# A recurrent branch whose heads overlap: a head's outputs are made inside the next head, and its squares are summed by two products of rounded numbers

## The chip, the cores and the metric

The kernel runs on one core of a Trainium2 chip as one program. The metric is the device time of one execution in microseconds (us), and lower is better. A core has a matrix engine (TensorE, "PE" in the profile), a vector engine (VectorE, "DVE"), an engine for functions of one operand (ScalarE, "ACT"), GpSimd ("POOL"), and SyncE ("SP"), whose queue starts most transfers here.

## The reference, cut to what matters

One encoder block on 512 tokens of width 1024: a mixer of two branches, then a retrieval layer (PEER) over 16384 small experts. The change is in the recurrent branch (HGRN2) of the mixer, which has 8 heads of 128 channels. Of its computation this much is touched:

```python
    o = o2[:B] + rev(o2[B:])                                  # both directions of the recurrence
    o = rmsnorm(o, hgrn_norm_g).reshape(B, L, HGRN_WIDTH)     # over the 128 channels of a head
    y_a = jnp.einsum('blc,cd->bld', (o * jax.nn.silu(og.astype(f32))).astype(xn.dtype), w_branch_a)

def rmsnorm(x, g):
    xf = x.astype(jnp.float32)
    y = xf * lax.rsqrt(jnp.mean(xf * xf, axis=-1, keepdims=True) + RMS_EPS)
    return (y * g.astype(jnp.float32)).astype(x.dtype)
```

The outputs `o` of a head are sums of products: scores with values within a chunk of 128 tokens, and queries with the states carried from the chunks before and after.

## The kernel before, in words

Tokens lie along the free axis (512 columns), channels along the 128 partitions. Products of full precision are made of three products of rounded numbers: `split` makes a rounded copy (`hi`, by ACT, line 94) and the rest (`lo`, by DVE, line 95), and `mm3` (lines 103, 104, 106) multiplies hi by hi, lo by hi and hi by lo. A projection of the input by one block of 128 columns of a weight is 24 such products of 128x512; this is called a block below. The first 16 of a block read `whi`, the last 8 `wlo`, and each of the two has two buffers, so the rest `wlo` of a weight can be written only when the block two before it has ended.

The function `hgrn` runs the recurrent branch. For every head `scores` makes the decays: two scans `Z` (699, 700), the keys and queries to the ends of the chunks `KE` and `QE` (719 to 724), transposes of the keys (733), states `S` (745, 752, 754), and, in two groups of levels, tiles `Dt`: a difference of `Z` (787, 788, DVE), its exponent (790, ACT), a product with keys and queries (769, 770, DVE). The products of each group (692, PE) give the score tiles `near` and `sct` (818, 825). Then `outputs` (835 to 841) multiplies the scores by the values `vh` and the queries by the states, into the PSUM tile `po`, and squares it; `normed` (847 to 851) adds up the squares over the channels by a product with a matrix of ones and scales the head. `sigmoids` of the next head is emitted within `scores`.

Beside this, PE makes five blocks per head, for the heads that come: `queried` and `forgets` (two each, run by `beside` between the steps of `scores`) and `values`. `weave` lets `beside` advance as `scores` yields costs. In the first step of `beside`, the norm of the head before and the transposes of the values (654) are emitted.

The code's order is not the order on the engines: when the program is built, a scheduler places the emitted instructions into one order per engine, with estimates of its own. On the chip every engine takes its instructions in that order and waits at one whose input or buffer isn't ready. So a change to what is emitted where can move instructions on all engines.

## Time and profile before

| | us |
|---|---|
| median of three runs | 2030.59 |
| lowest, highest | 2029.78, 2035.2 |
| profiled execution | 2031.44 |
| its span, first to last instruction | 2029.3 |
| recurrent branch, from head 0's outputs to the end of its last blocks | 405.6 to about 700 |
| busy in 405.6 to 700: PE, DVE, ACT | 289.9, 241.9, 209.8 |

A row of the profile names a line of the code, the engine, the operation, and the tiles as out<-in. In a list in order of time the first two numbers are the start and the length in us, and in brackets stands how long the engine was idle before it and whom it waited for. A product of two F32 tiles shows as two rows of half the work each, a product of rounded tiles as one row; the type reads f32 for both. The granted clock of TensorE is 1.00 in all of the stretch from 405.6 to 700.

### The profile page before, as it was taken

How to read it: one execution, taken by the hardware profiler on the slowest of the kernel's cores; microseconds unless marked ns; L12 is line 12 of the kernel's file. 1: busy time of each engine (PE TensorE's matmuls, PEld its weight loads, DVE VectorE, ACT ScalarE, POOL GpSimd, SP SyncE). 2: the span in 40 equal slices, each digit the busy share in tenths (PEclk: the TensorE clock that was granted, in tenths of full speed). 3: DMA queues.
4: the chain of work that ended last, by engine and by line, in shares of the span. 5: the costliest groups of instructions: out<-in, count | busy, mean ns of one | idle time of the engine just before them, and what ended most of it. 6: DMA issues, size and time to landing. Idle time of an engine off the chain costs nothing.

```text
span 2029.3 us, 32589 instructions
## 1 busy us (share of the span) xinstructions
PE 2005.8 (99%) x12553; PEld 1772.1 (87%) x12553; DVE 1656.0 (82%) x3016; ACT 983.7 (48%) x1473; POOL 555.4 (27%) x331
## 2 busy tenths in 40 slices
PE   8999999999999999999999999999999999999998
PEld 6788888888887888889999998888888888888887
DVE  6788863888988647979999968887897889898895
ACT  5555443777775623436767743333333323333333
POOL 0000000000000000000000027776766767766760
PEclk9999999999999999999999999999999999999999
DMA  5212113222212434214767998888988898998884
GB/s 187 94 53 68 63 58 108 84 74 74 69 70 73 138 144 146 99 68 154 228 203 234 276 339 327 327 333 317 362 312 315 319 361 338 367 346 328 325 306 156
DMA packets 160409, 418.08 MB, mean 206 GB/s; under 512 B 12890, under 2 KB 66012, under 8 KB 160126
## 3 DMA queue, kind: packets, MB, share of 16 engines
q1 hardware_dynamic: 115180, 263.58, 37.1%
q0 software_dynamic: 36864, 134.23, 18.0%
q10 hardware_dynamic: 8210, 18.19, 2.6%
q8 instruction: 98, 1.61, 0.3%
q14 instruction: 57, 0.47, 0.1%
HBM read 377.94 MB, written 38.01 MB: 205 GB/s over the span
## 4 chain that ended last, share of the span: by engine, by line
PE 94%; DVE 2%; issue 1%; DMA 1%; ACT 1%; POOL 0%; ACTq 0%; DVEq 0%; POOLq 0%
PE ps_mm L103 11%; PE ps_mm L104 10%; PE ps_mm L106 10%; PE ps_a L104 8%; PE ps_a L103 8%; PE ps_a L106 8%; PE acc L1132 8%; PE acc L1131 8%; PE acc L1133 8%; PE ps_g L1418 4%; PE ps_x L103 1%; PE ps_x L106 1%; PE ps_x L104 1%; PE ps_x L692 1%; PE ps_s L1263 1%
## 5 line engine op out<-in xcount | busy, mean ns | idle before, releaser
L103 PE MATMUL ps_a<-pxh,uh 128*128 128x384 f32 x1024 | 346.8, 339 | 0.4 <-ACT gact L983 0.4
L95 POOL TENSOR_TENSOR ul<-uraw,uh 128x1024 fp32r<-128x1024 f32 x70 | 186.4, 2663 | 576.1 <-PE ps_a L106 435.5
L104 PE MATMUL ps_a<-pxl,uh 128*128 128x384 f32 x1024 | 343.9, 336 | 0.0
L1132 PE MATMUL acc<-vl,gh 128*128 128x512 f32 x768 | 299.9, 390 | 0.0
L1131 PE MATMUL acc<-vh,gh 128*128 128x512 f32 x768 | 299.4, 390 | 0.0
L1133 PE MATMUL acc<-vh,gl 128*128 128x512 f32 x768 | 299.3, 390 | 0.0
L94 ACT CAST vh<-vraw 128x1024 fp32r<-128x1024 f32 x128 | 134.6, 1052 | 309.5 <-DMA vraw<-in_v 177.8
L103 PE MATMUL ps_mm<-xh,whi 128*128 128x512 f32 (+1 forms) x656 | 256.7, 393 | 0.4 <-ACT gt L265 0.4
L104 PE MATMUL ps_mm<-xl,whi 128*128 128x512 f32 (+1 forms) x656 | 252.6, 387 | 0.0
L1074 DVE SCALAR_TENSOR_TENSOR grow<-grow,xg 128x1024 f32<-128x1024 f32 x128 | 196.2, 1551 | 51.1 <-DMA grow<-in_u,gidx 50.7
L1086 DVE SCALAR_TENSOR_TENSOR xg<-grow,gw,xg 128x1024 f32<-128x1024 f32 x127 | 197.5, 1555 | 25.9 <-DMA grow<-in_v,gidx 23.5
L954 POOL IOTA iota<- 128x512 bf16 x1 | 1.2, 1189 | 764.3 <-PE ps_mm L106 764.3
L1045 POOL DMA_INDIRECT grow<-in_u,gidx x128 | 194.4, 1518 | 42.2 <-issue 23.4
L106 PE MATMUL ps_a<-pxh,ul 128*128 128x384 f32 x1024 | 198.3, 334 | 0.0
L103 PEld LDWEIGHTS ps_a<-pxh,uh 128*128 128x128 f32 x1024 | 192.4, 188 | 4.2 <-ACT gact L983 1.2
L104 PEld LDWEIGHTS ps_a<-pxl,uh 128*128 128x128 f32 x1024 | 192.7, 188 | 3.4
L95 DVE TENSOR_TENSOR wlo<-wraw,whi 128x1024 fp32r<-128x1024 f32 x112 | 136.5, 1220 | 71.2 <-ACT whi L94 41.5
L95 DVE TENSOR_TENSOR vl<-vraw,vh 128x1024 fp32r<-128x1024 f32 x128 | 182.5, 1426 | 5.3 <-ACT vh L94 5.3
L94 ACT CAST whi<-wraw 128x1024 fp32r<-128x1024 f32 x112 | 117.5, 1049 | 136.6 <-PE ps_mm L104 127.2
L94 ACT CAST uh<-uraw 128x1024 fp32r<-128x1024 f32 x128 | 134.5, 1051 | 101.3 <-PE ps_a L104 71.6
L1045 POOL DMA_INDIRECT grow<-in_v,gidx x128 | 173.3, 1354 | 37.0 <-issue 21.7
L106 PEld LDWEIGHTS ps_a<-pxh,ul 128*128 128x128 f32 x1024 | 179.3, 188 | 0.0
(420 smaller groups left out, 3988.8 us busy)
## 6 DMA issues: line engine op xcount, KB each, us to landing
uraw<-in_uT SPq DMA_DIRECT2D x128, 512.0 KB
vraw<-in_v SPq DMA_DIRECT2D x128, 512.0 KB
wraw<-in_w_in SPq DMA_DIRECT2D x80, 512.0 KB
Gd<-Gs SPq DMA_DIRECT2D x12, 2048.0 KB
gt<-Gd SPq DMA_DIRECT2D x32, 768.0 KB
kept<-gact ACTq DMA_DIRECT2D x22, 384.0 KB
gkept<-kept SPq DMA_DIRECT2D x22, 384.0 KB
wraw<-in_w_q SPq DMA_DIRECT2D x16, 512.0 KB
```

The lines of the kernel that those rows point to most:

```text
L94: nc.scalar.copy(hi, src)
L95: return (eng or nc.vector).tensor_sub(lo, src, hi).ins
L103: nc.tensor.matmul(out, ah, bh, start=(i == 0), stop=False)
L104: nc.tensor.matmul(out, *((al, bh) if late else (ah, bl)), start=False, stop=False)
L106: nc.tensor.matmul(out, *((ah, bl) if late else (al, bh)), start=False, stop=(stop and i == n - 1))
L1045: nc.gpsimd.indirect_dma_start(out=t, out_offset=None, in_=tab, in_offset=bass.IndirectOffsetOnAxis(ap=gidx[:, j : j + 1], axis=0))
L1074: nc.vector.scalar_tensor_tensor(t, t, 1.0, xg, op0=ALU.mult, op1=ALU.mult, accum_out=gdot[h][:, i : i + 1])
L1086: nc.vector.scalar_tensor_tensor(gacc, t, gw[h][:, i : i + 1], gacc, op0=ALU.mult, op1=ALU.add)
L1131: nc.tensor.matmul(acc[k][c], gh[:, ts_], vh[:, ds_], start=(r == 0), stop=False)
L1132: nc.tensor.matmul(acc[k][c], gh[:, ts_], vl[:, ds_], start=False, stop=False)
L1133: nc.tensor.matmul(acc[k][c], gl[:, ts_], vh[:, ds_], start=False, stop=(r == NK - 1))
L1418: nc.tensor.matmul(pg[:, q * P : q * P + P], own[:, q], rows[:, q], start=True, stop=True)
```

## The change

Three things change. First, `outputs` of a head is no longer emitted after `values` of the next one, but inside the next head, in the first step of `beside`, after that step's first block and before the transposes of the values. Second, the norm moves to the second step of `beside`. Third, the squares are split into a rounded part and a rest, which take a buffer of the ring of six `Dt` tiles, and the F32 product with ones becomes two products of rounded tiles with a constant `unit`. (`st[hd] = [raw]` is set earlier, which emits nothing.)

```diff
+    unit = cp.tile([P, P], F32R, name="unit")
+    nc.vector.memset(unit.bitcast(F32), 1.0)
...
         o2 = w1.tile([P, L], F32, name="o2")
         nc.scalar.activation(o2, po, AF.Square)
-        st[hd] += [po, o2]
+        o = w2.tile([P, 2, L], F32R, name="o2s", tag="Dt", bufs=6)
+        oh, ol = o[:, 0], o[:, 1]
+        split(nc, oh, ol, o2)
+        st[hd] += [po, oh, ol]
 
     def normed(hd):
-        so, po, o2 = st[hd][1], st[hd][-2], st[hd][-1]
+        so, (po, oh, ol) = st[hd][1], st[hd][-3:]
         pm = C.ps_x.tile([P, L], F32, name="ps_x")
-        nc.tensor.matmul(pm, C.ones, o2, start=True, stop=True)
+        nc.tensor.matmul(pm, unit, oh, start=True, stop=False)
+        nc.tensor.matmul(pm, unit, ol, start=False, stop=True)
...
     def beside(hd, work):
 
-        for i, c in enumerate(work):
+        for i in range(4):
+            if i == 1 and hd:
+                normed(hd - 1)
+            c = next(work)
             if i == 0:
                 if hd:
-                    normed(hd - 1)
+                    outputs(hd - 1)
                 transposed(hd)
             yield c
...
         weave(scores(hd), beside(hd, work), per)
         if hd < HEADS - 1:
             values(hd + 1)
-        outputs(hd)
+    outputs(HEADS - 1)
```

Lines from 618 on move down by two in the changed kernel, and from 845 on by more: the outputs are at 837, 839 and 841, the squares at 843, the products with `unit` at 852 and 853.

What this moves on the engines is shown for a middle head. On PE, before, the outputs (835 to 839) stand ahead of the transposes of the next head's keys (733), and the norm (847) comes one block after these:

```order
L839 MATMUL ps_x<-QE,S 128x128
L835 MATMUL ps_x<-sct,vh 128x128
L837 MATMUL ps_x<-QE,S 128x128
L733 MATMUL ps_x<-ident,KE 128x128 x6
L103 MATMUL ps_mm<-xh,whi 128x512
L104 MATMUL ps_mm<-xl,whi 128x512
```

In the changed kernel the transposes (735 now) stand four products into the next block:

```order
L103 MATMUL ps_mm<-xh,whi 128x512
L104 MATMUL ps_mm<-xl,whi 128x512
L735 MATMUL ps_x<-ident,KE 128x128 x6
L103 MATMUL ps_mm<-xh,whi 128x512
L104 MATMUL ps_mm<-xl,whi 128x512
```

and the outputs follow when that block has ended:

```order
L106 MATMUL ps_mm<-xh,wlo 128x512 x8
L837 MATMUL ps_x<-sct,vh 128x128
L841 MATMUL ps_x<-QE,S 128x128
L837 MATMUL ps_x<-sct,vh 128x128
L839 MATMUL ps_x<-QE,S 128x128
```

So the outputs of a head now come 20 products and six transposes after the keys of the next head are ready, instead of ahead of the transposes.

On DVE, before, the work on the first `Dt` tiles of a head stands around the product that ends `KE` (723):

```order
L709 TENSOR_TENSOR tot<-Z,lf 128x4
L780 COPY Dt<-KQ 128x512
L781 TENSOR_TENSOR Dt<-KQ,Dt 128x512
L95 TENSOR_TENSOR wlo<-wraw,whi 128x1024
L818 COPY_PREDICATED near<-masks,ps_x 128x256
L723 TENSOR_TENSOR KE<-KQ,KE 128x2x384
L818 COPY_PREDICATED near<-masks,ps_x 128x256
L724 TENSOR_TENSOR QE<-KQ,QE 128x768
L818 COPY_PREDICATED near<-masks,ps_x 128x256
L787 TENSOR_TENSOR Dt<-Z 128x8x64
L788 TENSOR_TENSOR Dt<-Z 128x2x4x64
L787 TENSOR_TENSOR Dt<-Z 128x16x32
```

Now two rests of weights stand ahead of it, and the rest of the squares (`o2s`) ahead of most of it:

```order
L677 MEMSET lf 128x2
L725 TENSOR_TENSOR KE<-KQ,KE 128x2x384
L726 TENSOR_TENSOR QE<-KQ,QE 128x768
L95 TENSOR_TENSOR wlo<-wraw,whi 128x1024 x2
L782 COPY Dt<-KQ 128x512
L789 TENSOR_TENSOR Dt<-Z 128x8x64
L95 TENSOR_TENSOR o2s<-o_4540,o2s 128x512
L783 TENSOR_TENSOR Dt<-KQ,Dt 128x512
L790 TENSOR_TENSOR Dt<-Z 128x2x4x64
L789 TENSOR_TENSOR Dt<-Z 128x16x32
```

Only a copy and one difference of the new head's `Dt` work are left between the keys and the rest of the squares; all else on the levels comes behind the squares of the head before. The order of the transfers on SP's queue and of the work on POOL is the same in both kernels.

## The prediction

> **What bounds the kernel now.** I read the busy shares first, then the recurrent branch by stretches from one head's outputs to the next, then PE's, DVE's and ACT's rows in order of time there. The page's first part, and five stretches of one head each (columns: stretch, length, then busy time and count of PE, PE's weight loads, DVE, ACT, POOL; clock; DMA):

> ```profile
> PE 2005.8 (99%) x12553; PEld 1772.1 (87%) x12553; DVE 1656.0 (82%) x3016; ACT 983.7 (48%) x1473; POOL 555.4 (27%) x331
> ...
> 442.54:479.50 36.96, 36.31 (x420) 29.90 (x420) 32.27 (x56) 27.72 (x43) 0.00 (x0) 1.00 0.21 72
> ...
> 590.45:627.33 36.88, 36.24 (x422) 29.81 (x421) 32.16 (x55) 27.64 (x43) 0.00 (x0) 1.00 0.22 73
> sum 184.79, PE 181.64 PEld 149.62 DVE 161.33 ACT 138.57 POOL 0.00; mean PE 36.33 PEld 29.92 DVE 32.27 ACT 27.71 POOL 0.00
> ```

> PE fills the whole kernel, so a change in one stage reaches the end whole. A head takes 36.96 us (184.79 / 5). DVE is busy for 32.27 of it: a second engine, 4.7 us below the bound. PE's rows at two head ends, and the wait named there:

> ```profile
> 402.36 1.97 PE L106 MATMUL ps_mm<-xh,wlo 128*128 128x512 f32 x8
> 405.61 0.49 PE L835 MATMUL ps_x<-sct,vh 128*128 128x128 f32 x2 [1.27 <-ACT sct L825]
> ...
> 439.94 1.98 PE L106 MATMUL ps_mm<-xh,wlo 128*128 128x512 f32 x8
> 442.54 0.49 PE L835 MATMUL ps_x<-sct,vh 128*128 128x128 f32 x2 [0.62 <-ACT sct L825]
> ...
> 444.65 0.39 PE L837 MATMUL ps_x<-QE,S 128*128 128x128 f32 x2
> 444.87 0.82 PE L733 MATMUL ps_x<-ident,KE 128*128 128x128 f32 x6
> 445.45 0.47 PE L103 MATMUL ps_mm<-xh,whi 128*128 128x512 f32 x1
> 445.76 0.40 PE L104 MATMUL ps_mm<-xl,whi 128*128 128x512 f32 x1
> 445.99 0.40 PE L103 MATMUL ps_mm<-xh,whi 128*128 128x512 f32 x1
> ...
> 451.01 1.02 PE L847 MATMUL ps_x<-o,ones 128*128 128x512 f32 x2
> 451.87 0.60 PE L654 MATMUL ps_x<-ident,vT 128*128 128x128 f32 x4
> ```

> Starts count, since PE overlaps its rows. Products of 128x512 start 0.23 apart (445.76, 445.99), so after eight from 439.94 the outputs could start at 441.77; they start at 442.54, a loss of 0.77. At head 0 it is 405.61 less 404.19, 1.42. The F32 product with ones takes 0.86 (451.01 to 451.87). A block takes 5.56 (445.45 to 451.01), the transposes of the keys 0.58, the outputs 2.50 from first start to last end (442.54 to 445.04).

> **The change part by part.** *Two rounded products for one of F32:* 2 x 0.23 for 0.86, so 0.40 less on PE, eight times. No row has `unit` as an operand; the nearest rows are the block's own products of this size, the other end is 0.86 each, as the F32 product (+0.86 per head). I take 0.23, the same kind.

> *Outputs one block later:* ACT's copies of `sct` are then long done, and the wait of 0.77 goes. Were PE alone the limit, a head would take 36.96 - 0.77 - 0.40 = 35.8.

> *What is late next:* DVE. In the new order its rows from the rest of the squares (`o2s`) of one head to the keys `KE` of the next stand without a gap to fill, and the next `o2s` can't start until those keys have gone through PE, a block, the outputs, and ACT. That is a loop, and I add up one turn of it. DVE's rows (groups of the stretch 442.5 to 479.5 with mean ns; rows of other stages for a split of 128x512; rows in order of time):

> ```profile
> L95 DVE TENSOR_TENSOR wlo<-wraw,whi 128x1024 fp32r<-128x1024 f32 x5 | 6.1, 1219 | 2.1 <-ACT whi L94 1.5 <-issue 0.7
> L787 DVE TENSOR_TENSOR Dt<-Z 128x512 f32<-128x512 f32 x6 | 4.1, 681 | 0.0
> L724 DVE TENSOR_TENSOR QE<-KQ,QE 128x768 f32<-128x768 f32 x1 | 0.9, 939 | 0.0
> L780 DVE COPY Dt<-KQ 128x512 f32<-128x512 f32 x1 | 0.5, 497 | 0.0
> ...
> L95 DVE TENSOR_TENSOR mgl<-gt,mgh 128x512 fp32r<-128x512 f32 x8 | 5.5, 685 | 1.1 <-ACT mgh L94 1.1
> L94 ACT CAST mgh<-gt 128x512 fp32r<-128x512 f32 x8 | 5.0, 620 | 12.2 <-DVE gt L306 12.2
> ...
> 442.13 0.68 DVE L788 TENSOR_TENSOR Dt<-Z 128x512 f32<-128x512 f32 x1
> 442.73 0.68 DVE L787 TENSOR_TENSOR Dt<-Z 128x512 f32<-128x512 f32 x1
> 443.33 0.68 DVE L788 TENSOR_TENSOR Dt<-Z 128x512 f32<-128x512 f32 x1
> 443.93 1.22 DVE L95 TENSOR_TENSOR wlo<-wraw,whi 128x1024 fp32r<-128x1024 f32 x1
> 445.07 0.68 DVE L769 TENSOR_TENSOR Dt<-KQ,Dt 128x512 f32<-128x512 f32 x1
> ```

> The starts lie 0.08 closer than the lengths (0.60 for a row of 0.68, 1.14 for the rest of a weight). The split adds 0.60 on DVE: 32.27 + 0.60 = 32.87 of work per head. Behind `KE` and so outside the run stand `QE` (0.86), two rests of weights (2.28), the copy (0.42) and one difference (0.60): 4.16. The run is 28.71 of work.

> [...]

> Waits inside the run, from ACT's rows:

> ```profile
> L779 ACT ACTIVATE Dt<-lf 128x512 f32<-128x512 f32 x1 | 0.9, 887 | 0.3 <-PE ps_x L692 0.3
> ...
> 445.84 0.59 ACT L841 ACTIVATE o<-ps_x 128x512 f32<-128x512 f32 x1
> ...
> 452.66 0.58 ACT L656 COPY vh<-ps_x 128x512 f32<-128x512 f32 x1
> 453.12 0.64 ACT L125 ACTIVATE hrs<-hrs 128x512 f32<-128x512 f32 x1
> ...
> 472.98 0.53 ACT L721 ACTIVATE KE<-Z 128x384 f32<-128x384 f32 x1 [1.54 <-DVE Z L700]
> 473.82 0.19 ACT L711 ACTIVATE edec<-tot 128x8 f32<-128x8 f32 x1
> 474.51 0.98 ACT L719 ACTIVATE KE<-Z,tot 128x128 f32<-128x128 f32 x3
> 478.63 0.82 ACT L825 COPY sct<-near 64x256 f32<-64x256 f32 x2 [2.26 <-DVE near L818]
> ```

> Behind the split, DVE's next row needs ACT's exponent of 0.89, which starts with the split and outlasts its step of 0.60 by some 0.2. Before `KE`, ACT now does an exponent (0.53), two copies of `sct` (0.82), `edec` (0.19) and three exponents (0.98) after the second scan, about 2.2 with steps overlapping, while DVE has only some 1.7 to do (a masked copy, two tiny ones, a rest of a weight at 1.14): 0.5 idle. With 0.2 for other handovers, 0.9. It could be 0.3, if the copies come early, or 1.6. The run is 29.6.

> From `KE` to the next `o2s`: PE's transposes 0.58, 20 products, which are a block less four (5.56 - 0.92 = 4.64), outputs 2.50, two handovers of 0.05: 7.8. ACT's square and copy of `vh` (0.46 to 0.48 apart by the starts above), the cast at 0.62 and a handover: 1.6. One turn: 29.6 + 7.8 + 1.6 = **39.0 to 39.1 us**, against 36.95 for the same turn before. I use 39.1. In those 9.4 us DVE has 4.16 of work and stands some 4.7 to 5.2 idle, first at the second rest of a weight (its buffer comes free when the block ends), then at `o2s`; differences of the new head, whose scans are done, are queued behind both. PE waits for DVE: it needs 35.8 and gets 39.1, so 3.3 per head, at the products of the second group of levels and at the transposes of the keys.

> Six turns, from head 0's outputs to head 6's; the rows of these before (the chain of waits):

> ```profile
> 405.61 0.49 PE ps_x L835 x2
> ...
> 627.33 0.49 PE ps_x L835 x2
> ```

> Before: 221.72, or 36.95 each. Added: 6 x (39.1 - 36.95) = 12.9. At the start the first outputs come later by transposes and a block, less the wait that goes: 0.58 + 5.56 - 1.42 = +4.7. At the end these lie ahead of head 6's outputs and need not follow: -6.1, and two norms are 0.40 shorter: -0.8. Head 7's outputs stay where they were. **Sum: 12.9 + 4.7 - 6.9 = +10.7 us.**

> *The rest:* setting `unit` is one small write by DVE at the head of the stage, where 0.7 of slack per head hides it, 0.2 at most if not. The split's 0.62 on ACT lies in the loop and is counted. Transfers of weights keep their order and start when buffers free, later with the loop; no transfer is added. The retrieval layer's work follows PE's and moves as a whole, since its gathers start from PE's projections there too.

> The profiled execution took 2031.44 (span 2029.3), 0.85 over the median of 2030.59: by it 2042.1, by the median 2041.3. I give the latter.

> **The rivals.** *PE stays the bound, faster.* If DVE's work for the second group were done when PE gets there, PE would lose nothing anew: waits of 1.42 and six of about 0.75 go, eight norms give 3.2, about -9: 2021.5. For it speaks PE's 99%; against it, that DVE has 4.7 idle per head before, and the new order alone takes that much between `KE` and `o2s`. It decides if a turn is under 35.8, 3.3 shorter than my sum. No wait in the run and none of the handovers make half of that. Chance 6%.

> *About even.* A turn of 36.95 + (6.9 - 4.7) / 6 = 37.3 leaves the time unchanged, and 36.3 to 38.3 keeps it within 6 us, 0.3% (about what a measurement of this kernel can tell from no change). That needs 0.8 to 2.8 less than my sum, for instance DVE's steps for rows on PSUM shorter, or the handovers less. Chance 8%.

> *ACT late as well.* ACT gains a cast (0.52 as a step) on 27.71 busy, and two weight casts stand back to back in front of the transposes' copies. If ACT's in-order queue held `KE` or the exponents 1 to 2 us more per turn, the time would be 6 to 12 us longer: 2047 to 2053. Against it: ACT has 9 us idle per head. Chance 7%. [...]

> **How the numbers follow.** My case, +6 to +16, has 78%, and its likeliest value is 2041.3. The waits in the run, 0.3 to 1.6 against 0.9, are -3.6 to +4.2 over six turns; with the handovers this is 2036 to 2047, where about 8 in 10 lie, the upper edge of the even case and the lower of ACT's included. Slower by over 0.3%: 78 + 7 + 1 = 86%; within 0.3%: 8%; faster: 6%.

> **What would show it.** Right: starts of the outputs (837) some 39 us apart in heads 1 to 6; PE's waits for `sct` gone; PE waiting for DVE at 694's second group (about 2 us a head) and at 735 (some 0.5); DVE idle before `wlo` and before `o2s`, together 4 to 5 us a head; the products with `unit` 0.23 apart; the retrieval layer as long as before. Wrong: no wait of PE at 694, which is the first rival; or DVE's idle time moved into the run, with ACT named, which is the third.

## The result, and the profile after

The changed kernel takes **2050.49 us** (median of 4 runs, 2049.99 to 2051.82) against 2032.22 for the kernel before in the same comparison. The ratio is 1.0095, with a 95% interval of 1.0081 to 1.0109: slower, as forecast, but by 18.3 us (medians) and not by 10.7. The profiled execution has a span of 2048.7 us against 2029.3 before, 19.4 more, and this is the amount taken apart here.

The engines' busy time (the page's first part) and six stretches, each from one head's outputs to the next head's (called a turn below; columns as in the prediction's first list):

```profile
PE 2014.0 (98%) x12553; PEld 1776.0 (87%) x12553; DVE 1659.8 (81%) x3025; ACT 989.7 (48%) x1481; POOL 557.5 (27%) x331
```

```profile
409.24:449.00 39.76, 36.70 (x421) 29.93 (x420) 33.41 (x56) 28.00 (x43) 0.00 (x0) 1.00 0.20 67
449.00:490.53 41.53, 39.21 (x421) 31.97 (x420) 33.38 (x56) 28.12 (x43) 0.00 (x0) 0.92 0.19 64
490.53:530.27 39.74, 36.76 (x422) 30.01 (x421) 33.30 (x56) 28.01 (x43) 0.00 (x0) 1.00 0.20 68
530.27:572.11 41.84, 39.65 (x421) 32.17 (x420) 33.38 (x56) 28.12 (x43) 0.00 (x0) 0.92 0.19 64
572.11:612.09 39.98, 36.88 (x421) 30.00 (x420) 33.31 (x56) 28.15 (x43) 0.00 (x0) 1.00 0.19 67
612.09:652.72 40.63, 38.04 (x421) 30.82 (x420) 33.38 (x55) 28.02 (x43) 0.00 (x0) 0.96 0.19 66
sum 243.48, PE 227.23 PEld 184.91 DVE 200.17 ACT 168.41 POOL 0.00; mean PE 37.87 PEld 30.82 DVE 33.36 ACT 28.07 POOL 0.00
```

Two things are to be seen. A turn now takes 39.7 to 40.0 us where the clock is full, 0.6 to 0.9 over the 39.1 that the prediction's loop through DVE has. And three of the six turns are longer still, and in just these the granted clock (third number from the end) is below 1.00. The forecast had no such term.

The 19.4 us between the spans are divided at three rows of PE: the transposes of head 0's keys, the first outputs and head 6's outputs. First the kernel before (its outputs at 405.61 and 627.33 stand in the prediction), then the changed one, both from PE's rows in order of time:

```profile
371.26 0.82 PE L733 MATMUL ps_x<-ident,KE 128*128 128x128 f32 x6
```

```profile
370.24 0.82 PE L735 MATMUL ps_x<-ident,KE 128*128 128x128 f32 x6
...
409.24 0.39 PE L837 MATMUL ps_x<-sct,vh 128*128 128x128 f32 x2
...
652.72 0.27 PE L837 MATMUL ps_x<-sct,vh 128*128 128x128 f32 x1
```

| piece | before, us | after, us | measured | forecast |
|---|---|---|---|---|
| up to head 0's transposes | 371.26 | 370.24 | -1.0 | 0 |
| from there to the first outputs | 34.35 | 39.00 | +4.65 | +4.7 |
| six turns | 221.72 | 243.48 | +21.76 | +12.9 |
| from head 6's outputs to the end | 1401.97 | 1395.98 | -6.0 | -6.9 |
| sum | 2029.3 | 2048.7 | +19.4 | +10.7 |

So 8.9 us more than forecast lie in the six turns; the other differences, -1.0 and +0.9, nearly cancel.

**An undisturbed turn.** DVE's rows in order of time (brackets: idle time ahead, and what ended it), from the outputs of 490.53 to those of 530.27:

```profile
490.79 1.23 DVE L95 TENSOR_TENSOR wlo<-wraw,whi 128x1024 fp32r<-128x1024 f32 x1 [3.10 <-PE ps_mm L106]
491.93 0.50 DVE L782 COPY Dt<-KQ 128x512 f32<-128x512 f32 x1
492.35 0.68 DVE L789 TENSOR_TENSOR Dt<-Z 128x512 f32<-128x512 f32 x1
494.59 0.69 DVE L95 TENSOR_TENSOR o2s<-o,o2s 128x512 fp32r<-128x512 f32 x1 [1.56 <-ACT o2s L94]
495.37 0.69 DVE L783 TENSOR_TENSOR Dt<-KQ,Dt 128x512 f32<-128x512 f32 x1
495.98 0.68 DVE L790 TENSOR_TENSOR Dt<-Z 128x512 f32<-128x512 f32 x1
...
498.63 0.69 DVE L771 TENSOR_TENSOR Dt<-KQ,Dt 128x512 f32<-128x512 f32 x1 [0.16 <-ACT Dt L792]
...
513.81 0.69 DVE L771 TENSOR_TENSOR Dt<-KQ,Dt 128x512 f32<-128x512 f32 x1 [0.31 <-ACT Dt L792]
...
523.97 0.96 DVE L725 TENSOR_TENSOR KE<-KQ,KE 128x768 f32<-128x768 f32 x1 [0.80 <-ACT KE L721]
```

DVE stands idle for 3.10 and 1.56 between one head's keys and the rest of its predecessor's squares, 4.7 together, while the new head's differences stand queued behind. From `o2s` at 494.59 to the end of `KE` at 524.93 the run takes 30.34. Then PE needs 5.34 until the outputs start (530.27). The outputs before had started at 490.53; ACT's square follows them 2.44 later and the rest of the squares another 1.62:

```profile
492.97 0.60 ACT L843 ACTIVATE o<-ps_x 128x512 f32<-128x512 f32 x1 [3.00 <-PE ps_x L839]
493.46 0.58 ACT L658 COPY vh<-ps_x 128x512 f32<-128x512 f32 x1
493.93 0.63 ACT L94 CAST o2s<-o 128x512 fp32r<-128x512 f32 x1
```

30.34 + 5.34 + 2.44 + 1.62 = 39.74, the whole turn. PE waits at the second group of products (694) and at the keys (735), as these waits of PE from 400 to 700 us show (total, times, longest):

```profile
PE ps_x L694 <- ACT raw L637: 6.7, 5, 1.5
PE ps_x L694 <- DVE Dt L772: 4.3, 6, 0.7
PE ps_x L735 <- DVE KE L725: 1.8, 3, 0.6
```

The wait for `sct` of before is gone. The profile puts the longest of these waits down to ACT's copy of `raw`, since that ends last, 0.06 before the products start (in the sixth head it names another copy of ACT's, `ga`). But in each of the six heads these products start 0.15 after DVE's row 772 has ended, which makes their operand, and so do those of the second line, put down to DVE. Both are waits for DVE.

**A disturbed turn.** PE's rows at the second group of products in the turn from 449.00 to 490.53:

```profile
470.65 1.52 PE L106 MATMUL ps_mm<-xh,wlo 128*128 128x512 f32 x6
473.72 0.46 PE L694 MATMUL ps_x<-Dt 128*32 128x32 f32 x32 [1.55 <-ACT raw L637]
474.92 0.66 PE L694 MATMUL ps_x<-Dt 128*32 128x32 f32 x32 [0.74 <-DVE Dt L772]
...
478.37 0.63 PE L103 MATMUL ps_mm<-xh,whi 128*128 128x512 f32 x1
478.80 0.63 PE L104 MATMUL ps_mm<-xl,whi 128*128 128x512 f32 x1
...
481.67 0.39 PE L103 MATMUL ps_mm<-xh,whi 128*128 128x512 f32 x1
481.89 0.39 PE L104 MATMUL ps_mm<-xl,whi 128*128 128x512 f32 x1
```

Behind the waits of 1.55 and 0.74, products of 128x512 start 0.43 apart (478.37, 478.80), and from 481.67 on 0.22 apart again. The clock's records in the trace say the same: half from 474.68 for 6.83 us, from 556.60 for 6.83, and from 638.52 for 3.41, full otherwise until the very end of the kernel. The first of these stretches, as a row of the kind shown above:

```profile
474.68:481.51 6.83, 6.56 (x76) 4.88 (x77) 6.03 (x12) 2.91 (x5) 0.00 (x0) 0.50 0.23 79
```

The kernel before has no half clock in this stage.

### The profile page after: what moved, and what is told of

It is laid out like the page before. It is cut to its first block, busy times and chain, and to the rows that moved or that the text cites. A ratio compares the mean times of both kernels' runs of the same rounds, so it can differ in the third digit from the quotient of the medians.

```text
span 2048.7 us, 32590 instructions
## 1 busy us (share of the span) xinstructions
PE 2014.0 (98%) x12553; PEld 1776.0 (87%) x12553; DVE 1659.8 (81%) x3025; ACT 989.7 (48%) x1481; POOL 557.5 (27%) x331
## 3 DMA queue, kind: packets, MB, share of 16 engines
q1 hardware_dynamic: 115180, 263.58, 36.5%
q8 instruction: 99, 1.62, 0.3%
## 4 chain that ended last, share of the span: by engine, by line
PE 91%; ACT 5%; DVE 3%; DMA 1%; issue 0%; SPq 0%; ACTq 0%; DVEq 0%
PE ps_mm L103 9%; PE ps_mm L104 9%; PE ps_mm L106 9%; PE ps_a L104 9%; PE ps_a L103 9%; PE ps_a L106 9%; PE acc L1141 9%; PE acc L1140 9%; PE acc L1142 9%; PE ps_g L1427 4%; PE ps_x L103 1%; PE ps_x L106 1%; PE ps_x L104 1%; PE ps_s L1272 1%; ACT Dt L792 1%; PE ps_x L747 1%
## 5 line engine op out<-in xcount | busy, mean ns | idle before, releaser
L95 POOL TENSOR_TENSOR ul<-uraw,uh 128x1024 fp32r<-128x1024 f32 x70 | 190.1, 2716 | 578.5 <-PE ps_a L106 433.9
L103 PE MATMUL ps_a<-pxh,uh 128*128 128x384 f32 x1024 | 346.8, 339 | 0.3 <-ACT gact L992 0.3
L104 PE MATMUL ps_a<-pxl,uh 128*128 128x384 f32 x1024 | 343.9, 336 | 0.0
L94 ACT CAST vh<-vraw 128x1024 fp32r<-128x1024 f32 x128 | 134.5, 1051 | 266.7 <-DMA vraw<-in_v 136.4
L103 PE MATMUL ps_mm<-xh,whi 128*128 128x512 f32 (+1 forms) x656 | 259.8, 398 | 1.6 <-ACT whi L94 0.9
L104 PE MATMUL ps_mm<-xl,whi 128*128 128x512 f32 (+1 forms) x656 | 255.9, 392 | 0.0
L1083 DVE SCALAR_TENSOR_TENSOR grow<-grow,xg 128x1024 f32<-128x1024 f32 x128 | 190.1, 1505 | 51.3 <-DMA grow<-in_u,gidx 51.0
L1095 DVE SCALAR_TENSOR_TENSOR xg<-grow,gw,xg 128x1024 f32<-128x1024 f32 x127 | 201.7, 1588 | 30.9 <-DMA grow<-in_v,gidx 29.2
L1054 POOL DMA_INDIRECT grow<-in_u,gidx x128 | 193.0, 1508 | 39.7 <-issue 22.2
L106 PE MATMUL ps_a<-pxh,ul 128*128 128x384 f32 x1024 | 198.3, 334 | 0.0
L104 PEld LDWEIGHTS ps_a<-pxl,uh 128*128 128x128 f32 x1024 | 192.7, 188 | 3.5
L103 PEld LDWEIGHTS ps_a<-pxh,uh 128*128 128x128 f32 x1024 | 192.4, 188 | 3.7 <-ACT gact L992 0.6
L95 DVE TENSOR_TENSOR wlo<-wraw,whi 128x1024 fp32r<-128x1024 f32 x112 | 136.6, 1220 | 71.1 <-PE ps_mm L106 40.0
L94 ACT CAST uh<-uraw 128x1024 fp32r<-128x1024 f32 x128 | 134.5, 1051 | 114.6 <-PE ps_a L104 82.8
L106 PEld LDWEIGHTS ps_a<-pxh,ul 128*128 128x128 f32 x1024 | 179.3, 188 | 0.0
L95 DVE TENSOR_TENSOR vl<-vraw,vh 128x1024 fp32r<-128x1024 f32 x128 | 175.8, 1374 | 3.2 <-ACT vh L94 3.2
L94 ACT CAST whi<-wraw 128x1024 fp32r<-128x1024 f32 x112 | 116.7, 1047 | 124.6 <-PE ps_mm L104 112.6
```

Source lines behind the costliest of these rows:

```text
L94: nc.scalar.copy(hi, src)
L95: return (eng or nc.vector).tensor_sub(lo, src, hi).ins
L103: nc.tensor.matmul(out, ah, bh, start=(i == 0), stop=False)
L104: nc.tensor.matmul(out, *((al, bh) if late else (ah, bl)), start=False, stop=False)
L106: nc.tensor.matmul(out, *((ah, bl) if late else (al, bh)), start=False, stop=(stop and i == n - 1))
L1054: nc.gpsimd.indirect_dma_start(out=t, out_offset=None, in_=tab, in_offset=bass.IndirectOffsetOnAxis(ap=gidx[:, j : j + 1], axis=0))
```

## The experiments

Theory: the loss is the loop of the prediction, and it closes (its members wait for one another all the way round) because two things come together. `o2s` takes a buffer of the ring of six that the `Dt` tiles use, and buffers of a ring are handed out in the order of the code, so the new head's `Dt` work stands behind `o2s` on DVE; and the outputs, a block later than before, make `o2s` late. The idle time that this gives PE lowers the clock (to half for 6.83, 6.83 and 3.41 us, by the records above), on top. Rivals: one part alone costs the time, or the clock alone does.

### One part alone: the split, with the outputs at their old place

```diff
-        for i in range(4):
-            if i == 1 and hd:
-                normed(hd - 1)
-            c = next(work)
+        for i, c in enumerate(work):
...
-                    outputs(hd - 1)
+                    normed(hd - 1)
...
-    outputs(HEADS - 1)
+        outputs(hd)
```

> Two rounded products and the split, with outputs and norm left where they were before the change. Theory (the loss needs both parts: outputs that stand behind a block, and the rest of the squares in the ring of Dt tiles, which puts the new head's Dt work behind it on DVE): a turn of some 36.1 us, PE full, 5 to 9 us faster than before. Rival 1 (the split costs, since DVE and ACT each get a row more per head): 3 to 12 us slower. Rival 2 (the move alone costs): 3 us faster, eight norms at 0.40.

Measured: 2024.91 us (2023.49 to 2026.03) against 2030.03; ratio 0.9974 (0.9965 to 0.9983), faster. Five of the six turns take 36.3 to 36.4, one 37.8, and the six 219.73 against 221.72 before, with a full clock:

```profile
402.32:622.05 219.73, 215.39 (x2521) 179.60 (x2519) 197.39 (x335) 168.47 (x259) 0.00 (x0) 1.00 0.22 73
```

### The other part alone: the outputs a block later, squares summed whole

From the changed kernel, with the sum of the kernel before:

```diff
-        o = w2.tile([P, 2, L], F32R, name="o2s", tag="Dt", bufs=6)
-        oh, ol = o[:, 0], o[:, 1]
-        split(nc, oh, ol, o2)
-        st[hd] += [po, oh, ol]
+        st[hd] += [po, o2]
...
-        nc.tensor.matmul(pm, unit, oh, start=True, stop=False)
-        nc.tensor.matmul(pm, unit, ol, start=False, stop=True)
+        nc.tensor.matmul(pm, C.ones, o2, start=True, stop=True)
```

> Outputs inside the next head and the norm in its second step, but with the one F32 product with ones and no split. Theory (both parts needed): the wait for the score copies goes, a turn of some 36.3 us, 4 to 6 us faster than before, clock at 1.00 throughout. Rival 1 (the split costs): also 4 to 6 faster. Rival 2 (the move alone costs, since the outputs come a block later in the loop): 10 to 20 us slower.

Measured: 2025.25 us (2024.57 to 2026.36); ratio 0.9977 (0.9968 to 0.9986), faster. The turns are 36.3 to 36.5, and the start (39.03) and the end (1395.9) as in the changed kernel. The six turns:

```profile
409.23:627.19 217.96, 217.87 (x2522) 179.93 (x2521) 192.65 (x329) 166.26 (x252) 0.00 (x0) 1.00 0.22 74
```

So neither part costs anything by itself: each gives about 5 us, and both together cost 18 to 19.

### Both parts, the split in another buffer

```diff
-        o = w2.tile([P, 2, L], F32R, name="o2s", tag="Dt", bufs=6)
+        o = w1.tile([P, 2, L], F32R, name="o2s", tag="KE")
```

> The changed kernel with one edit: the split squares take the buffer of KE in place of one of the six Dt buffers; same instructions. Theory (the ring of Dt hands out buffers in the order of the code, so new Dt work can't go ahead of the split squares): DVE's Dt work moves ahead again, a turn of about 36 us, 6 to 9 us faster than before, no wait of PE at the second group, clock at 1.00. Rival (the outputs' place behind a block and DVE's extra row make the loop long, wherever the buffer is): as the changed kernel, 17 to 20 us slower than before.

Measured: 2024.34 us (2023.73 to 2026.21); ratio 0.9975 (0.9964 to 0.9985): 5.7 us faster than before, a little under the 6 to 9 expected. Six turns take 217.30 with a full clock, so this one line is worth 26.6 us by the spans (2022.1 and 2048.7). DVE's rows at the same place in the program show why:

```profile
473.05 0.95 DVE L725 TENSOR_TENSOR KE<-KQ,KE 128x768 f32<-128x768 f32 x1
...
475.45 0.50 DVE L782 COPY Dt<-KQ 128x512 f32<-128x512 f32 x1
475.87 0.67 DVE L783 TENSOR_TENSOR Dt<-KQ,Dt 128x512 f32<-128x512 f32 x1
...
485.38 0.68 DVE L772 TENSOR_TENSOR Dt<-KQ,Dt 128x512 f32<-128x512 f32 x1
485.98 0.67 DVE L95 TENSOR_TENSOR o2s<-o,o2s 128x512 fp32r<-128x512 f32 x1
```

Between the keys and `o2s` DVE now works for 12 us without a gap, on 14 rows of the new head's `Dt` among others (the first and the last two are shown), where the changed kernel had two of them and 4.7 us idle. The loop is open; no row became cheaper.

### The clock alone: PE kept busy in its waits

Five rounded products ahead of the second group in heads 1 to 6; the group overwrites what they put in its bank, so their values are not used:

```diff
             bank = C.ps_x.tile([P, L], F32, name="ps_x")
+            if 0 not in levels and 0 < hd < HEADS - 1:
+                for _ in range(5):
+                    nc.tensor.matmul(bank, xh[:, 0, :P], xh[:, 1], start=True, stop=True)
```

> The changed kernel with five more products of rounded 128x512 tiles (about 1.15 us) put on PE ahead of the second group of levels in heads 1 to 6, into the PSUM tile that the group then overwrites; their values are not used. Theory (PE's idle stretch there lowers the granted clock to half for 3.4 to 6.8 us in three heads, which costs 4.5 us in all): clock at 1.00 throughout, every turn about 39.8 us, 3 to 5 us faster than the changed kernel, 14 to 16 us slower than before. Rival (the clock has another cause, or the products are not hidden): as the changed kernel or up to 7 us slower than it, 19 to 26 us slower than before.

Measured: 2045.67 us (2044.54 to 2046.15); ratio 1.0076 (1.0062 to 1.0089). The clock is full throughout, and the turns are 39.76, 39.77, 39.79, 39.78, 39.77 and 39.77. Their sum, in one stretch:

```profile
409.13:647.76 238.63, 226.95 (x2551) 185.30 (x2550) 200.04 (x335) 168.16 (x258) 0.00 (x0) 1.00 0.20 67
```

That is 4.85 below the changed kernel's 243.48, with 30 products more on PE. So the half clock costs 4.85 us, and 39.77 is the loop's own turn (238.63 / 6): PE's five products per head lie in its waits and cost nothing.

The same with two products in place of five:

> The changed kernel with two 128x512 rounded products in heads 1 to 6, issued to PE ahead of the second group, whose values nobody uses; the run with five of them held the clock at 1.00. They leave PE idle for some 1.8 of 3.4 us at that place. If the clock falls only where PE idles for about two thirds of such a stretch (2.2 us, as in the changed kernel), it stays at 1.00 and the kernel takes 2045 to 2047 us with turns of 39.8. If half a stretch is enough, some turns are again 0.8 to 2 us longer with clock records of 0.5, and the time is 2048 to 2051 us.

Measured: 2048.26 us (2047.8 to 2050.96); ratio 1.0090 (1.0076 to 1.0104). The mean clock is 0.96 in four turns, which is what 3.41 us at half make of 40.5 us (1 - 0.5 x 3.41 / 40.5), and these take 40.4 to 40.6; the other two have 1.00 and take 39.77. So the first theory of that run, that two thirds of a stretch must be idle, falls. In the changed kernel's records a drop lasts 3.413 us or 6.827, twice as long, and the drops begin 81.92 us apart, 24 times 3.413; in this run the first two and the last two of the four begin 40.96 apart, 12 times 3.413. So I divided the time into stretches of 3.41 that end where the drops begin, and read PE's busy time. The changed kernel (three that a drop follows, then the one with least PE work that none follows):

```profile
471.26:474.67 3.41, 1.37 (x37) 0.79 (x35) 3.09 (x6) 3.41 (x6) 0.00 (x0) 1.00 0.00 0
553.18:556.59 3.41, 1.44 (x66) 0.83 (x64) 3.09 (x7) 3.41 (x5) 0.00 (x0) 1.00 0.00 0
635.10:638.51 3.41, 1.14 (x65) 0.79 (x64) 3.13 (x6) 3.41 (x5) 0.00 (x0) 1.00 0.00 0
512.21:515.62 3.41, 1.88 (x39) 1.30 (x37) 3.10 (x6) 3.41 (x5) 0.00 (x0) 1.00 0.00 1
```

and the one with two products (the busiest of the four that a drop follows, and one that none follows):

```profile
474.68:478.09 3.41, 1.51 (x67) 1.24 (x67) 3.41 (x7) 3.41 (x5) 0.00 (x0) 1.00 0.00 0
553.16:556.57 3.41, 2.08 (x40) 1.38 (x38) 3.09 (x6) 3.41 (x5) 0.00 (x0) 1.00 0.00 0
```

In the changed kernel, from 400 to 700 us, a drop begins behind the three stretches with PE busy for 1.14, 1.37 and 1.44, and behind none of the others, which have 1.88 or more. In the run with two products the four ahead of a drop have 1.34 to 1.51, and the one of 2.08 has none behind it. At what busy time between 1.51 and 1.88 the clock begins to fall isn't shown, nor why two of the seven drops last two stretches and the others one.

### The outputs ahead of the next head's first block

The third way to open the loop leaves the ring alone and issues the outputs earlier:

```diff
+            if i == 0 and hd:
+                outputs(hd - 1)
             c = next(work)
             if i == 0:
-                if hd:
-                    outputs(hd - 1)
                 transposed(hd)
```

> The changed kernel with one step moved: a head's outputs are issued ahead of the next head's first block of work, so that its squares and their split into rounded parts come before that block in program order, with the ring of six buffers left as it is. If the loss comes from the order in which the squares' split and the next head's Dt work take buffers of the ring, with the outputs late, then the outputs 8 us earlier on PE open the loop: turns of 35.8 to 36.3 us between outputs in place of 39.8, no wait of PE for Dt, granted clock 1.00, 2020 to 2025 us. If any use of that ring by the squares stretches the turn, wherever the outputs stand, the turns stay above 38 us and the time above 2040 us.

Measured: **2018.43 us** (2018.29 to 2019.62) against 2029.69; ratio 0.9943 (0.9929 to 0.9956), faster than both kernels and than the 2020 to 2025 expected. The six turns in one stretch:

```profile
404.46:619.16 214.70, 214.13 (x2523) 179.82 (x2521) 196.47 (x335) 168.72 (x258) 0.00 (x0) 1.00 0.22 75
```

PE is busy for 214.13 of 214.70. `o2s` keeps its ring, and on DVE it still stands ahead of most of the new head's `Dt` rows; but the block is no longer between keys and outputs. Taking its 4.64 us out of a loop of 39.77 leaves 35.1, less than the 35.7 of work that PE has per turn (214.13 / 6), so PE is the bound again.

With the norm issued right after the first block as well:

> As the run before, and the two rounded sums of a head's squares are issued right after the next head's first block and not after its second. If the outputs' place sets the turn, this one is within 1 us of the run before over the whole kernel (2020 to 2025 us). If the sums have to stand a block later for their split to be done in time, PE waits 1 us or more per head for the split's rest, and the kernel is 5 us or more slower than the run before.

Measured: 2019.88 us (2019.52 to 2020.52); ratio 0.9949 (0.9936 to 0.9963). Five of six turns take 35.6 to 35.7, as in the run before, and PE has no wait for the split's rest. The six together:

```profile
405.02:619.86 214.84, 214.21 (x2523) 179.87 (x2521) 196.44 (x335) 168.62 (x258) 0.00 (x0) 1.00 0.23 75
```

That is 214.84 against 214.70: in the turns the norm's place doesn't matter. The 1.4 us between the medians is more than the 1 us expected, and the two kernels' times hardly overlap. Of the 0.8 us between the profiled spans, 0.6 lies ahead of head 0's transposes, where the two kernels do the same; why wasn't followed.

And with the outputs early, but the squares summed whole:

> The kernel with the outputs ahead of the next head's first block (fifth run), but the squares summed up whole by one F32 product with ones, as before the change: no split, no rounded products. If PE is the bound once the loop is open, each of the eight norms costs PE 0.40 us more, and the kernel takes 3 us more than the fifth run: 2021 to 2023 us, with turns of 35.9 to 36.2 us. If the split's cast and rest take back on ACT and DVE what PE gains, the time is that of the fifth run, 2018 to 2019 us.

Measured: 2025.54 us (2024.95 to 2026.83) against 2029.55; ratio 0.9979 (0.9970 to 0.9988). The split is worth more than the 3 us expected: 6.1 between the spans (2024.0 and 2017.9), of which 3.05 lie in the six turns, 0.8 between head 0's transposes and the first outputs, and 2.6 behind head 6's outputs, less 0.2 ahead of all these. By PE's rows the norm's place is 0.42 longer per head, near the 0.40 that the prediction took; for eight norms, 3.4. The stretch from the keys' transposes to the second output product is 0.26 longer per head too, and the waits of 1.4 (for `vh`) and 0.6 (for `sct`) come once each. Why the transposes and the first output products take 0.26 more there wasn't followed.

### A buffer of its own, and a ring of five

```diff
-        sg = w2.tile([P, 2, L], F32, name="sg", tag="Dt", bufs=6)
+        sg = w2.tile([P, 2, L], F32, name="sg", tag="Dt", bufs=5)
...
-                Dt = w2.tile([P, 2, L], F32, name="Dt", bufs=6)
+                Dt = w2.tile([P, 2, L], F32, name="Dt", bufs=5)
...
-        o = w2.tile([P, 2, L], F32R, name="o2s", tag="Dt", bufs=6)
+        o = w2.tile([P, 2, L], F32R, name="o2s", bufs=1)
```

> The changed kernel with a buffer of its own for the squares' split, and the ring that held it cut from six buffers to five (the space has to come from somewhere). If what costs is that the split stands between a head's Dt buffers in the order in which they are handed out, the turns fall from 39.8 to 36.5 to 38 us though a buffer of Dt is gone, and the time is 2026 to 2036 us. If the number of buffers that Dt has to itself is what counts, five are short as well, and the turns stay at 39 us or more with 2044 us or more.

Measured: 2030.46 us (2028.85 to 2031.25) against 2029.69; ratio 1.0002 (0.9993 to 1.0011), no change. Turns are 36.9 and then 37.4, with a full clock. One buffer less for `Dt`, and still 19.6 us below the changed kernel by the span (2029.1): most of the time goes with the place in the ring's order, not with the number of buffers. Against the run with `KE`'s buffer (2022.1) it is 7.0 longer, so a ring of five is not free either, as far as these two runs can be compared. What is left shows in these two waits of PE (400 to 700 us; total, times, longest):

```profile
PE ps_x L853 <- DVE o2s L95: 3.9, 6, 0.8
PE ps_x L694 <- DVE Dt L772: 2.7, 6, 0.5
```

## Why the prediction was right and wrong

The step that failed is the clock: the sum gave the new idle time of PE no price beyond the waits themselves, and it cost another 4.85 us. A second term, DVE's waits within its run, was too small, by 4.0 us over six turns. With the clock kept full (the run with five filling products) the kernel takes 2045.67 us, inside the forecast 2036 to 2047; with the drops of the clock it is outside.

- **The loop through DVE: right.** It is the mechanism, at the place and with the members named. The three runs that break it, by another buffer, by a ring without `o2s`, and by earlier outputs, bring turns of 35.6 to 37.4; each part alone doesn't close it.
- **The legs: right.** 7.8 on PE and 1.6 on ACT were forecast; 7.78 and 1.62 are measured.
- **DVE's run: mis-sized.** Forecast were 28.71 of work and 0.9 of waits, 29.6; measured 30.34. By the rows above, the waits inside are 0.80 ahead of `KE` (0.5 forecast), 0.16 and 0.31 for exponents of differences (only 0.2 was set aside for all other handovers), 0.09 behind `o2s`; and a row that has waited (it starts 0.09 to 0.80 behind the end of the row ahead, by the rows above) does not start the 0.08 early that the others do. Together (1.36 of waits and five times 0.08) that is about 1.76, twice the term, and the work is 28.6. The forecast turn was 39.1, and the loop's own is 39.77: six times 0.67 is 4.0 us. The third rival had put 1 to 2 us per turn of such waits on ACT with 7%; the truth lay between. The measured 2050.49 falls into that rival's 2047 to 2053, but by luck: ACT's waits alone would not have brought it there, as the run with a full clock shows.
- **DVE's rows a full length apart: not seen.** The 86% counts 1% for such rows, an estimate of the author's (2065 us, from some 50 rows a turn at 0.08 each) that no run shows. In the changed kernel a row of 0.69 at 495.37 is followed by one at 495.98, 0.61 later; before the change, rows of 0.68 start 0.60 apart.
- **The clock: left out.** The sum set three turns to the same length as the others. The half clock makes the six 4.85 longer, which the run with five filling products took back. The prediction had forecast the idle time itself (2 us per head at the second group; measured 11.0 in the two lines above for 694 and 13.3 with two single waits there, or 2.2 per head), and stopped there: idle time of an engine off the limit was taken as free. In the kernel before, the longest wait that the prediction quotes from this stage is 1.27, and the clock is full there, so the trace of before has no case of it. In the changed kernel PE was busy for 1.14 to 1.44 of the 3.41 us ahead of each drop, and its longest single wait there was 1.55.
- **Start and end.** The start came as forecast (+4.65 for +4.7). The end gave 6.0 for 6.9; what kept the 0.9 wasn't followed. The stage begins 1.0 earlier for no reason in the change; the runs spread over 369.4 to 371.5 there.
- **The sum.** 10.7 + 4.0 (waits) + 4.85 (clock) + 0.9 (end) - 1.0 = 19.45, against 19.4 in the spans. The range had taken the waits up to 4.2 over six turns, and 4.0 came; the clock came on top.
- **Two rounded products at 0.23 each: nearly.** PE's rows in the changed kernel:

```profile
494.35 0.39 PE L104 MATMUL ps_mm<-xl,whi 128*128 128x512 f32 x1
494.61 0.50 PE L852 MATMUL ps_x<-o2s,unit 128*128 128x512 f32 x1
494.95 0.40 PE L103 MATMUL ps_mm<-xh,whi 128*128 128x512 f32 x1
...
495.87 0.39 PE L853 MATMUL ps_x<-o2s,unit 128*128 128x512 f32 x1
496.10 0.40 PE L103 MATMUL ps_mm<-xh,whi 128*128 128x512 f32 x1
```

  They stand apart inside a block. The first occupies 0.34 until the next product starts, the second 0.23: 0.57 for the 0.86 of before. It changed nothing here, as PE had 2 us of waits per head.
- **PE alone at 35.8: right, as a bound.** The first rival's turn was not reached here, but with the outputs early it is: 35.6 to 35.7.

## What to carry to other kernels

A tile that borrows a buffer of another tile's ring also takes that ring's order: what is allocated after it, stands behind it, and if it is produced late, everything behind is late as well: 39.77 us a turn here, against 36.2 (217.30 / 6) in `KE`'s buffer. Before a borrowed buffer is used, follow the loop from its producer round to its next use and add it up; here, opening it at any one link was enough, and the fastest kernel was the one that issues the outputs one block earlier. And where a forecast finds new idle time on TensorE, price the clock as well as the wait; here it was 4.85 us.
